# A decoder trunk's second and output products in blocks of four outputs, on 62 placements of their tiles

## The chip, the cores and the metric

The kernel runs on one core of one Trainium2 chip. The metric is the device time of one execution in microseconds: 2296.33 us is the median of three runs before the change (2295.15, 2296.38, 2296.33). The core has a matrix engine (TensorE, PE in the profile, with its weight loads listed apart as PEld), a vector engine (DVE), a scalar engine (ACT), a general engine (POOL) and SyncE, whose queue issues most DMAs. Each works through its own instructions in order and waits for the others on semaphores.

## The reference, cut to what matters

Two layers on 256 tokens of width 2048, in float32. Layer 0 has a convolution module, layer 1 an attention; each is followed by a gated feed-forward (ConvFFN).

```python
def conv_ffn(h, up_w, dw_w, dw_b, down_w):
    u = causal_depthwise_conv(h @ up_w, dw_w, dw_b)
    gt, val = jnp.split(u, 2, axis=-1)
    return (jax.nn.silu(gt) * val) @ down_w

for i in range(DEPTH):
    ...
    y = conformer_conv_module(...) if i % 2 == 0 else stick_breaking_mixer(h, sb_qkv_w[j], sb_o_w[j])
    x = x + gate * y
    ...
    x = x + gate * conv_ffn(h, ffn_up_w[i], ffn_dw_w[i], ffn_dw_b[i], ffn_down_w[i])
return rms_norm(x, final_norm_g)
```

The two products that matter here are the one with `down_w` (5632 to 2048, the "second product" of a feed-forward) and the one with the attention's output weights (2048 to 2048, the "output product").

## The kernel before, in words

Activations lie transposed: a tile has 128 features on the partitions and 256 tokens along them. An activation is kept as two halves whose sum is the float32 value, a high one (`hh`, `gh`, `oh`) and a low one (`hl`, `gl`, `ol`), in one tile with the second half some elements behind the first. A weight block of 128 by 128 is split likewise on the chip into `wh` (a cast on ACT, L244) and `wl` (a subtraction on DVE, L248), eight blocks (a piece) at a time, from `raw`, which SyncE's queue loads. Four pairs `wh`, `wl` are in rotation.

A product is a list of steps (output block, input tile), made by `plan` and packed in that order on the host. A step of the form used here has two matmuls: L299 takes `wh` against both halves of a tile at once (512 columns, through an access pattern of two runs of 256 that lie a fixed distance apart), L300 takes `wl` against the high half (256 columns). The high half's sums stand in the first 256 columns of a PSUM bank, the low half's in the rest. One output block in each second product (`LAST`, number 15) uses three matmuls of 256 instead (L304 to L306).

`plan(nbs, kts, first)` runs the first `first` outputs together, tile by tile, so that each tile is used by `first` steps running; the last four tiles (`stagger`) then go output by output, so that the outputs end four steps apart. All further outputs come one after the other, each over all its tiles. For the second products, each in two halves of 22 tiles (`down00`, `down01` in layer 0, `down10`, `down11` in layer 1), and the output product (`o`, 16 tiles), `first` is 4: four outputs together, then twelve alone.

Accumulators are PSUM banks of a pool `acc` with five buffers (tile `ps`), which serve in rotation; a bank is free again when its output is drained. In a second product the drain `down_done` copies the second half on ACT (L1024), adds it to the residual `x` on POOL (L1025) and adds the first half on DVE (L1029), which ends the bank's use. Output 14 takes both halves on DVE (L1027, L1029). In the output product both are DVE's (L1210). Where a normalization follows (`down01`, `o`, `down11`), a square (ACT, L402), a running sum of squares (POOL, L406), and either a pair of casts for the next product (ACT L458, DVE L459) or a scale (ACT, L1035) belong to the drain. The mean of squares is made on TensorE from that sum and from the last square (L410, L411).

Beside all this run reductions of the modulation weights on DVE (L338, 128 by 2048 elements each, input `mraw`), paced by pieces of the products; they occur in layer 0's second products and not in those of layer 1. A scheduler puts the instructions of each engine into a fixed order before the run, by its own estimates, with the drains at a raised priority; the order on an engine need not be that of the code.

`halved` allocates a tile for two halves. `PAIRS` gives the distance of the halves and the size of a tile, in elements of 4 bytes. By it all `g` tiles (inputs of the second products, 23 buffers) start at the same place in a stretch of 256 bytes, byte 160, and their second halves 32 bytes further on; `o` tiles alternate between the bytes 160 and 32; the `h` tiles of the other products, from `h_tiles`, rotate through 32, 96, 160 and 224.

Of the kernel before, what the change touches and what calls it, by code (L numbers as in the profile page):

```python
# [11 lines left out]
F32R = mybir.dt.float32r  # L12
# [4 lines left out]
P = 128  # L17
# [7 lines left out]
LATE_POOL, LATE_PE = 10, 8  # L25
PRODUCTS = 11

PAIRS = {"z": (264, 528, 0), "g0": (264, 576, 0), "g1": (264, 576, 0), "o": (264, 544, 0)}
HEAD = 16
UBUFS = 9  # L30
M0 = 6
# [10 lines left out]
QUIET = 6  # L42
PRIORITY = 100
MORE_MODS = 2


def plan(nbs, kts, first, stagger=4):

    seq = []
    if first > 1:  # L50
        head, nbs = nbs[:first], nbs[first:]
        s = min(stagger, len(kts) // 2)
        seq += [(n, k) for k in kts[:len(kts) - s] for n in head]
        seq += [(n, k) for n in head for k in kts[len(kts) - s:]]
    return seq + [(n, k) for n in nbs for k in kts]


class Cfg:
    def __init__(self, D, T, H, F, CW, FW):
        self.D, self.T, self.H, self.F, self.CW, self.FW = D, T, H, F, CW, FW  # L60
        KD = self.KD = D // P
        KF = self.KF = F // P
        self.GH = 4
        self.rows0 = min(ROWS, KD // 4)

        def columns(items):
            cols, n = {}, 0
            for name, k in items:
                cols[name] = (n, n + k)
                n += k  # L70
            return cols, n

        items = []
        items += [("mix_g1", KD), ("mix_b1", 3 * KD)]
        for i in range(2):
            items += [(f"ffn_g{i}", KD), (f"ffn_b{i}", 3 * KD)]
        for i in range(2):
            items += [(f"fdw{i}", 2 * KF * FW), (f"fdb{i}", 2 * KF)]
        items += [("fin_g", KD)]
        self.cols, self.ncols = columns(items)  # L80
        items = [("c", KD), ("mix_g0", KD), ("mix_b0", 3 * KD), ("pw1_b", 2 * KD), ("cdw", KD * CW), ("cdb", KD), ("ln_g", KD), ("ln_b", KD),
                 ("pw2_b", KD)]
        self.ccols, self.nccols = columns(items)

        kd = list(range(KD))
        pl = {}
        pairs = [n for j in range(KD) for n in (j, j + KD)]
        pl["pw1"] = plan(pairs, kd, min(HEAD, 2 * KD), 0)
        pl["pw2"] = plan(kd, kd, 8)
        self.halves = [list(range(KF // 2)), list(range(KF // 2, KF))]  # L90
        for i in range(2):
            for h, js in enumerate(self.halves):
                up = [n for j in js for n in (j, j + KF)]
                if h == 0:
                    pl[f"up{i}0a"] = plan(up[:FIRST], kd, FIRST, STAGGER)
                    pl[f"up{i}0b"] = plan(up[FIRST:], kd, 2, STAGGER)
                else:
                    pl[f"up{i}1a"] = plan(up[:2], kd, 1)
                    pl[f"up{i}1b"] = plan(up[2:], kd, 1)
                pl[f"down{i}{h}"] = plan(kd, js, 4)  # L100
        GH = self.GH
        for g in range(H // GH):
            hs = list(range(g * GH, (g + 1) * GH))
            qk = [n for h in hs for n in (h, H + h)]
            pl[f"qk{g}a"] = plan(qk[:FIRST], kd, FIRST if g == 0 else 1, STAGGER)
            pl[f"qk{g}b"] = plan(qk[FIRST:], kd, 1)
            pl[f"v{g}"] = [(2 * H + h, k) for k in kd for h in hs]
        pl["o"] = plan(kd, list(range(H)), 4)
        self.plans = pl
        order = ["pw1", "pw2", "up00a", "up00b", "up01a", "down00", "up01b", "down01"]  # L110
        for g in range(H // GH):
            order += [f"qk{g}a", f"v{g}"] if g == 0 else [f"v{g}", f"qk{g}a"]
            order.append(f"qk{g}b")
        self.order = order + ["o", "up10a", "up10b", "up11a", "down10", "up11b", "down11"]
# [3 lines left out]
def hybrid_trunk(ctx: ExitStack, tc: tile.TileContext, cfg: Cfg, io: dict):  # L118
    nc = tc.nc
    D, T, H = cfg.D, cfg.T, cfg.H  # L120
# [243 lines left out]
    HP = T + 8  # L364
# [7 lines left out]
    def h_pairs():  # L372
        return [pairs[k] for k in range(KD)]

    ahead_of = {kind: v[2] for kind, v in PAIRS.items()}

    def halved(pool, kind, name):

        low, size, _ = PAIRS[kind]
        at = ahead_of.pop(kind, 0)  # L380
        v = pool.tile([P, at + size], F32R, name=name)[:, at:at + 2 * low].rearrange("p (a t) -> p a t", a=2)[:, :, :T]
        return v[:, 0], v[:, 1], v

    def split_act(t, hh, hl, bias=None):
# [120 lines left out]
    with ExitStack() as cv:  # L505
# [342 lines left out]
        for c in range(KD + 1):  # L848
# [6 lines left out]
            if c > 0:  # L855
                old = [(c - 1, k) for k in vector_taps(c - 1)[split(c - 1):]]
                n = max(len(taps), len(old))
# [3 lines left out]
            for s in range(nd):  # L861
# [17 lines left out]
                if c == KD and s == 0:  # L879
                    low = split_next(later=True)  # L880
# [100 lines left out]
    def ffn(i, entry, out):  # L981
# [3 lines left out]
        with ExitStack() as fs:  # L985
            gpool = fs.enter_context(tc.tile_pool(name=f"g{i}", bufs=1))
            if i == 0:
                more["pool"] = fs.enter_context(tc.tile_pool(name="mods", bufs=MORE_MODS))
            gh, gl, gb = [None] * KF, [None] * KF, [None] * KF
# [60 lines left out]
    def mods1(parts, ring):  # L1050
# [26 lines left out]
        while ahead:  # L1077
# [4 lines left out]
    fill.append(mods1((("ffn0", 2), ("mix1", 1), ("mix1", 0), ("mix1", 2), ("ffn1", 1), ("ffn1", 0)),  # L1082
                      lambda: [mpool] * 3 + [more["pool"]] * MORE_MODS))
    entry1 = Entry("mix1")
# [143 lines left out]
    for h in range(2):  # L1228
        t = slice(h * HT, (h + 1) * HT)
        nc.vector.reciprocal(rs[:, t], std[:, t])  # L1230
        v = mpool.tile([P, D], F32, name="mraw")[:, :KD * HT].rearrange("p (k t) -> p k t", k=KD)
# [129 lines left out]
```

## Time and profile before

| what | value |
|---|---|
| median of three runs | 2296.33 us |
| the profiled execution | 2295.19 us, of which its span 2293.5 us |
| granted clock of TensorE, mean | 0.998 |
| second products (330 steps and 22 of `LAST` each) | 665.7 to 787.9, 1023.1 to 1149.6, 1801.0 to 1923.2, 2158.4 to 2280.6 us |
| output product (256 steps) | 1449.0 to 1540.8 us |
| DMA share in 665.7 to 787.9 | 0.94 |
| DMA share in 2158.4 to 2280.6 | 0.51 |

A row of a timeline gives start and length in us, engine, line, operation and what it writes from what. Names are without buffer numbers. A matmul's length is longer than its share of TensorE, since the next one starts before its end; the distance from start to start is its cost. In a row of windows stand the window, its length, busy time of PE, PEld, DVE, ACT and POOL with the count of instructions in brackets, TensorE's granted clock, the DMA share and GB/s.

### The profile page before, as it was taken

The numbers are of one execution on the slowest core, as the hardware profiler recorded it, in microseconds if no ns is written. First come the engines' busy times: TensorE is split into PE (matmuls) and PEld (weight loads), VectorE is DVE, ScalarE is ACT, GpSimd is POOL, SyncE is SP. The second block draws the span as 40 slices with busy tenths as digits, with TensorE's granted clock in tenths as the row PEclk, the third lists the DMA queues.
The fourth block names the chain that finished last, engine by engine and source line by source line (L and its number), as shares of the span: only waits on it lengthen the run. The fifth ranks groups of instructions, "written<-read, shape, count | busy, mean of one in ns | idle before, by whom it ended". The sixth has DMA issues, their size and how long they took to land.

```text
span 2293.5 us, 37839 instructions
## 1 busy us (share of the span) xinstructions
PE 2259.2 (99%) x14466; PEld 2011.7 (88%) x14466; DVE 1790.7 (78%) x2504; ACT 1218.8 (53%) x1930; POOL 410.7 (18%) x534
## 2 busy tenths in 40 slices
PE   7999999999999999999999999999999999999997
PEld 5888678999998999998898888888888888888887
DVE  7689968989998899999975555779899755777654
ACT  2056655755544455554465555657555544555553
POOL 4058713200003100003411100112000010000031
PEclk9999999999999999999999999999999999999999
DMA  9988798789899989888755555566777566656663
GB/s 397 417 336 305 273 363 349 290 298 337 332 350 340 338 329 340 336 333 307 277 185 159 165 174 169 170 189 235 240 282 277 193 191 188 190 185 186 192 192 111
DMA packets 139144, 603.16 MB, mean 263 GB/s; under 512 B 15441, under 2 KB 15569, under 8 KB 115153
## 3 DMA queue, kind: packets, MB, share of 16 engines
q1 hardware_dynamic: 120242, 464.42, 57.7%
q0 software_dynamic: 18720, 136.32, 16.0%
q8 instruction: 113, 1.85, 0.3%
q14 instruction: 69, 0.57, 0.1%
HBM read 598.58 MB, written 2.10 MB: 262 GB/s over the span
## 4 chain that ended last, share of the span: by engine, by line
PE 86%; DVE 7%; DMA 4%; ACT 1%; issue 1%; POOL 0%; DVEq 0%; SPq 0%; ACTq 0%; POOLq 0%
PE ps L299 32%; PE ps L300 16%; PE ps L304 9%; PE ps L305 9%; PE ps L306 8%; PE ps L694 5%; DMA mraw<-in_mt_mix 3%; DVE mraw L338 3%; DVE wl L248 2%; PE ps L1184 1%; PE ps L1185 1%; PE ps L1186 1%; PE ps L586 1%; DMA mraw<-in_mt_ffn 1%; DMA raw<-in_w_pw 1%
## 5 line engine op out<-in xcount | busy, mean ns | idle before, releaser
L248 DVE TENSOR_TENSOR wl<-raw,wh 128x1024 fp32r<-128x1024 f32 x688 | 848.0, 1239 | 299.5 <-ACT wh L244 297.7
L244 ACT CAST wh<-raw 128x1024 fp32r<-128x1024 f32 x688 | 719.0, 1047 | 660.6 <-PE ps L299 283.5
L299 PE MATMUL ps<-h,wh 128*128 128x512 f32 x1760 | 619.0, 394 | 0.0
L300 PE MATMUL ps<-h,wl 128*128 128x256 f32 x1760 | 494.0, 281 | 0.0
L299 PE MATMUL ps<-g,wh 128*128 128x512 f32 x1320 | 458.6, 393 | 0.0
L304 PE MATMUL ps<-h,wh 128*128 128x256 f32 (+1 forms) x1504 | 422.0, 281 | 0.0
L305 PE MATMUL ps<-h,wh 128*128 128x256 f32 (+1 forms) x1504 | 420.8, 280 | 0.0
L306 PE MATMUL ps<-h,wl 128*128 128x256 f32 (+1 forms) x1504 | 419.2, 279 | 0.1
L299 PEld LDWEIGHTS ps<-h,wh 128*128 128x128 f32 x1760 | 330.5, 188 | 74.5
L338 DVE CUSTOM_DVE_ANT_0 mraw<-mraw,csr 128x2048 f32<-128x2048 f32 x152 | 350.4, 2305 | 31.2 <-DMA mraw<-in_mt_mix 28.5
L300 PE MATMUL ps<-g,wl 128*128 128x256 f32 x1320 | 367.8, 279 | 2.3 <-DVE wl L248 2.2
L300 PEld LDWEIGHTS ps<-h,wl 128*128 128x128 f32 x1760 | 332.7, 189 | 0.2
L299 PEld LDWEIGHTS ps<-g,wh 128*128 128x128 f32 x1320 | 247.8, 188 | 57.8
L305 PEld LDWEIGHTS ps<-h,wh 128*128 128x128 f32 x1504 | 284.8, 189 | 0.1
L306 PEld LDWEIGHTS ps<-h,wl 128*128 128x128 f32 x1504 | 282.8, 188 | 0.7 <-DVE wl L248 0.7
L304 PEld LDWEIGHTS ps<-h,wh 128*128 128x128 f32 x1504 | 282.6, 188 | 0.1
L300 PEld LDWEIGHTS ps<-g,wl 128*128 128x128 f32 x1320 | 248.1, 188 | 4.1 <-DVE wl L248 4.1
L694 PE MATMUL ps<-h,raw 128*128 128x256 f32 x832 | 188.6, 382 | 0.0
L694 PEld LDWEIGHTS ps<-h,raw 128*128 128x128 f32 x832 | 158.0, 191 | 28.1 <-issue 5.8
L1025 POOL TENSOR_TENSOR x<-x,t 128x256 f32<-128x256 f32 x56 | 70.0, 1250 | 530.1 <-ACT t L1024 529.8
L1003 DVE SCALAR_TENSOR_TENSOR t<-t,par 128x254 f32<-128x254 f32 (+1 forms) x184 | 88.8, 483 | 46.6 <-ACT t L1000 43.7
L734 DVE SCALAR_TENSOR_TENSOR auxb<-u,cpar,auxb 128x256 f32<-128x256 f32 x297 | 121.6, 483 | 4.5 <-ACT auxb L718 3.7
(272 smaller groups left out, 2735.0 us busy)
## 6 DMA issues: line engine op xcount, KB each, us to landing
raw<-in_w_down SPq DMA_DIRECT2D x176, 512.0 KB, 4.3
mraw<-in_mt_ffn POOLq DMA_DIRECT2D x64, 1024.0 KB, 6.7
raw<-in_w_pw SPq DMA_DIRECT2D x96, 512.0 KB, 8.0
mraw<-in_mt_mix POOLq DMA_DIRECT2D x48, 1024.0 KB, 7.9
raw<-in_w_up01b SPq DMA_DIRECT2D x84, 512.0 KB, 6.8
raw<-in_w_up11b SPq DMA_DIRECT2D x84, 512.0 KB, 3.6
raw<-in_w_up00b SPq DMA_DIRECT2D x80, 512.0 KB, 6.1
raw<-in_w_up10b SPq DMA_DIRECT2D x80, 512.0 KB, 4.7
```

What stands on the lines that cost most here:

```text
L244: nc.scalar.copy(wh[:, :n], v[:, :n])
L248: nc.vector.tensor_tensor(wl[:, :n], v[:, :n], wh[:, :n].bitcast(F32), op=ALU.subtract)
L299: nc.tensor.matmul(o, wh[:, c], both[kt], start=first, stop=False, skip_group_check=True)
L300: nc.tensor.matmul(o[:, :T], wl[:, c], xh[kt], start=False, stop=left[nb] == 0, skip_group_check=True)
L304: nc.tensor.matmul(o, wh[:, c], xh[kt], start=first, stop=False, skip_group_check=halves > 0)
L305: nc.tensor.matmul(o, wh[:, c], xl[kt], start=False, stop=False, skip_group_check=halves > 0)
L306: nc.tensor.matmul(o, wl[:, c], xh[kt], start=False, stop=left[nb] == 0, skip_group_check=halves > 0)
L338: nc.vector.tensor_tensor_reduce(out=v, in0=v, in1=csr, scale=1.0, scalar=0.0, op0=ALU.mult, op1=ALU.add, accum_out=macc[:, nb:nb + 1])
L694: nc.tensor.matmul(banks[j][:, nb // KD * T:(nb // KD + 1) * T], w[:, b * P:(b + 1) * P], hf[kt], start=first, stop=left[j] == 0, skip_gro ...
L734: nc.vector.scalar_tensor_tensor(conv_ps[j], us[j % UBUFS][:, k:k + T], tap(j, k), conv_ps[j], op0=ALU.mult, op1=ALU.add)
L1003: nc.vector.scalar_tensor_tensor(y[:, s:], ps[:, :T - s], w(k), y[:, s:], op0=ALU.mult, op1=ALU.add)
L1025: nc.gpsimd.tensor_tensor(xs[nb], xs[nb], t, op=ALU.add)
```

## The change

`fours` cuts the outputs into blocks of four and plans each block with `first=4`: every block now is what only the first one was. `circuit` orders the 64 pairs (start of the first half, start of the second, in steps of 32 bytes within 256) into a closed round in which each pair begins where the one before ended; `START` deals 23 of them to layer 0's `g` tiles, 16 to the `o` tiles and 23 to layer 1's `g` tiles. Tiles that follow each other in memory follow each other in the round. The weights' packed order follows the plans; their bytes and the number of instructions stay. Lines of the changed kernel are 15 higher than before up to the tile code, 23 after it: L299 is L314, L248 is L263, L338 is L353, L1029 is L1052.

```diff
-PAIRS = {"z": (264, 528, 0), "g0": (264, 576, 0), "g1": (264, 576, 0), "o": (264, 544, 0)}
+START = {"g0": (0, 5, 5), "g1": (23, 5, 5), "o": (46, 5, 5)}
...
+def fours(nbs, kts):
+    return [x for i in range(0, len(nbs), 4) for x in plan(nbs[i:i + 4], kts, 4)]
+
+def circuit(n=8, at=5):
+    ends, path, out = {i: [(i + 3 * k) % n for k in range(n)] for i in range(n)}, [at], []
+    while path:
+        if ends[path[-1]]:
+            path.append(ends[path[-1]].pop())
+        else:
+            out.append(path.pop())
+    return list(zip(out[:-1], out[1:]))
...
-                pl[f"down{i}{h}"] = plan(kd, js, 4)
+                pl[f"down{i}{h}"] = fours(kd, js)
...
-        pl["o"] = plan(kd, list(range(H)), 4)
+        pl["o"] = fours(kd, list(range(H)))
...
-    ahead_of = {kind: v[2] for kind, v in PAIRS.items()}
+    edges, opened = circuit(), {}
     def halved(pool, kind, name):
-        low, size, _ = PAIRS[kind]
-        at = ahead_of.pop(kind, 0)
-        v = pool.tile([P, at + size], F32R, name=name)[:, at:at + 2 * low].rearrange("p (a t) -> p a t", a=2)[:, :, :T]
+        if kind == "z":
+            v = pool.tile([P, 2 * HP], F32R, name=name).rearrange("p (a t) -> p a t", a=2)[:, :, :T]
+            return v[:, 0], v[:, 1], v
+        first, at, base = START[kind]
+        n = first + int(name[1:])
+        p, q = edges[n]
+        ahead = 8 * ((p - at) % 8) if n == first else 0
+        low = T + 8 * ((q - p) % 8)
+        size = (ahead + low + T + 7) // 8 * 8
+        t = pool.tile([P, size], F32R, name=name)
+        v = bass.AP(tensor=t.tensor, offset=t.offset + ahead, ap=[list(t.ap[0]), [low, 2], [1, T]])
         return v[:, 0], v[:, 1], v
```

On TensorE, at the end of the first block of the last product (`down11`), before: the last step of output 3 (`ps_22061`), then output 4 alone (`ps_22328`) on the tiles g22, g0, g1.

```order
L299 MATMUL ps_22061<-g20_22042,wh_22206 128x512
L300 MATMUL ps_22061<-g20_22042,wl_22207 128x256
L299 MATMUL ps_22328<-g22_18667,wh_22228 128x512
L300 MATMUL ps_22328<-g22_18667,wl_22229 128x256
L299 MATMUL ps_22328<-g0_19842,wh_22228 128x512
L300 MATMUL ps_22328<-g0_19842,wl_22229 128x256
L299 MATMUL ps_22328<-g1_19952,wh_22228 128x512
```

The same place in the changed kernel, where outputs 4 to 7 (`ps_22328`, `ps_22331`, `ps_22334`, `ps_22337`) open:

```order
L315 MATMUL ps_22061<-g20_22042,wl_22207 128x256
L314 MATMUL ps_22328<-g22_18667,wh_22228 128x512
L315 MATMUL ps_22328<-g22_18667,wl_22229 128x256
L314 MATMUL ps_22331<-g22_18667,wh_22228 128x512
L315 MATMUL ps_22331<-g22_18667,wl_22229 128x256
L314 MATMUL ps_22334<-g22_18667,wh_22228 128x512
L315 MATMUL ps_22334<-g22_18667,wl_22229 128x256
L314 MATMUL ps_22328<-g0_19842,wh_22228 128x512
L315 MATMUL ps_22328<-g0_19842,wl_22229 128x256
L314 MATMUL ps_22331<-g0_19842,wh_22228 128x512
L314 MATMUL ps_22337<-g22_18667,wh_22228 128x512
```

`ps_22328` takes the bank that is fifth in rotation; `ps_22331`, `ps_22334` and `ps_22337` take the banks of the block's first three outputs, one after the other. The scheduler has put the fourth one's first matmul behind four steps and one L314; a matmul of the fourth output on the first tile thus stands behind some of the second tile.

On DVE, the drains of outputs 4 and 5 of the last product before, with splits of weights between them:

```order
L1029 SCALAR_TENSOR_TENSOR x_82<-ps_22328,v_ffn1_101,x_82 128x256
L248 TENSOR_TENSOR wl_22401<-raw_22345,wh_22400 128x1024
L248 TENSOR_TENSOR wl_22423<-raw_22367,wh_22422 128x1024
L248 TENSOR_TENSOR wl_22445<-raw_22398,wh_22444 128x1024
L1029 SCALAR_TENSOR_TENSOR x_82<-ps_22393,v_ffn1_101,x_82 128x256
```

And in the changed kernel, outputs 4 to 7:

```order
L1052 SCALAR_TENSOR_TENSOR x_82<-ps_22328,v_ffn1_101,x_82 128x256
L263 TENSOR_TENSOR wl_22565<-raw_22502,wh_22564 128x1024
L1052 SCALAR_TENSOR_TENSOR x_82<-ps_22331,v_ffn1_101,x_82 128x256
L1052 SCALAR_TENSOR_TENSOR x_82<-ps_22334,v_ffn1_101,x_82 128x256
L263 TENSOR_TENSOR wl_22603<-raw_22524,wh_22602 128x1024
L1052 SCALAR_TENSOR_TENSOR x_82<-ps_22337,v_ffn1_101,x_82 128x256
```

Drains that stood three splits apart now stand together, in the order that the first block has in both kernels.

On DVE in layer 0's first second product (`down00`), outputs 4 and 5 before (`ps_7138`, `ps_7202`), where the rows `ISA` are a reduction and the reading of its sum:

```order
L1029 SCALAR_TENSOR_TENSOR x_82<-ps_7138,v_ffn0_99,x_82 128x256
L338 ISA mraw_6972,macc_102<-mraw_6972,csr_83 128x2048
L338 ISA macc_102 128x1
L248 TENSOR_TENSOR wl_7213<-raw_7158,wh_7212 128x1024
L248 TENSOR_TENSOR wl_7235<-raw_7180,wh_7234 128x1024
L248 TENSOR_TENSOR wl_7257<-raw_7210,wh_7256 128x1024
L1029 SCALAR_TENSOR_TENSOR x_82<-ps_7202,v_ffn0_99,x_82 128x256
```

In the changed kernel, outputs 4 to 7 (`ps_7138`, `ps_7141`, `ps_7144`, `ps_7147`):

```order
L1052 SCALAR_TENSOR_TENSOR x_82<-ps_7138,v_ffn0_99,x_82 128x256
L263 TENSOR_TENSOR wl_7382<-raw_7324,wh_7381 128x1024
L1052 SCALAR_TENSOR_TENSOR x_82<-ps_7141,v_ffn0_99,x_82 128x256
L353 ISA mraw_7158,macc_102<-mraw_7158,csr_83 128x2048
L353 ISA macc_102 128x1
L263 TENSOR_TENSOR wl_7412<-raw_7346,wh_7411 128x1024
L1052 SCALAR_TENSOR_TENSOR x_82<-ps_7144,v_ffn0_99,x_82 128x256
L1052 SCALAR_TENSOR_TENSOR x_82<-ps_7147,v_ffn0_99,x_82 128x256
```

A reduction and a split stand between the drains of the block's second and third output.

## The prediction

> **What bounds the kernel.** I read the page first: the busy shares, then the chain that ended last.
>
> ```profile
> span 2293.5 us, 37839 instructions
> PE 2259.2 (99%) x14466; PEld 2011.7 (88%) x14466; DVE 1790.7 (78%) x2504; ACT 1218.8 (53%) x1930; POOL 410.7 (18%) x534
> PE 86%; DVE 7%; DMA 4%; ACT 1%; issue 1%; POOL 0%; DVEq 0%; SPq 0%; ACTq 0%; POOLq 0%
> ```
>
> TensorE sets the end: it is busy 99% of the span and is 86% of the chain. A microsecond in which it waits, or by which its matmuls get longer, is a microsecond of the whole, unless the same stage already holds a wait that swallows it. Next I read the groups by line in three stretches: the second feed-forward's second half of up-products (1923.4 to 2158.3 us, moving tiles h), its last second product (2158.4 to 2272.8, tiles g) and the output product behind its first block (1474.3 to 1540.8, tiles o).
>
> ```profile
> L299 PE MATMUL ps<-h,wh 128*128 128x512 f32 x672 | 235.2, 393 | 0.0
> ...
> L299 PE MATMUL ps<-g,wh 128*128 128x512 f32 x330 | 114.5, 393 | 0.0
> ...
> L299 PE MATMUL ps<-o,wh 128*128 128x512 f32 x192 | 66.6, 391 | 0.0
> ```
>
> TensorE has no gap there, so busy time over count is the cost of a step (L299 and L300 together): 350 ns on h, 347 on g, 347 on o. The program's addresses go with it: all g tiles start at one place (byte 160 of 256, second half 32 further), h tiles rotate through four places, o tiles through two. So the cost depends a little on the tile. The windows of the two second products of the first layer and of the last one show what else is near its limit:
>
> ```profile
> 665.70:780.10 114.40, 114.40 (x663) 99.85 (x662) 98.08 (x98) 50.91 (x59) 28.25 (x32) 1.00 0.93 348
> 1023.10:1141.80 118.70, 116.41 (x663) 100.36 (x662) 113.47 (x125) 60.37 (x90) 44.59 (x40) 1.00 0.81 295
> 2158.40:2272.80 114.40, 114.40 (x662) 99.86 (x661) 58.62 (x60) 62.48 (x88) 27.79 (x27) 1.00 0.55 167
> ```
>
> In the second row DVE is busy 113.5 of 118.7 us and TensorE idles 2.3 us. In the third DVE has half its time free.
>
> **The change, part by part.** No instruction is added or removed; weights arrive in another packed order, as many bytes. Three things move.
>
> **1. What a step costs on 62 tiles.** 4 products of 330 steps go from one place to 62; so do the 192 output steps behind the first block: 1512 steps that cost 347 ns now. Most run four times on one tile. Before shows such runs in the first block of the output product; here are the starts of o6, o7 and of what follows:
>
> ```profile
> 1458.81 0.40 PE L299 MATMUL ps<-o,wh 128*128 128x512 f32 x1
> ...
> 1460.19 0.40 PE L299 MATMUL ps<-o,wh 128*128 128x512 f32 x1
> ...
> 1461.62 0.34 PE L1131 MATMUL auxb<-mh,tri_r 128*128 128x384 f32 x1
> ```
>
> Four steps on o6 (start 160, as g) take 1.38 us, 345 each; four on o7 (start 32) take 1.43, 357.5 each. Only these two repeated places and the rotating four are seen, of 62, so the mean is bounded from both sides by them: 345 gives 1512 x -2 ns = -3.0 us, 357.5 gives +15.9. I take 352, the middle of g's 347 and o7's 357.5: 1512 x 5 ns = **+7.6 us**.
>
> The Trainium skill, "TensorE: Matmul & The Clock Gate", section "Back-to-back issue gap", gives a warm matmul N/2.4 + 2.5 ns with no term for where the operand lies: 215.8 and 109.2, an estimate of 325 ns a step on every tile. By that rule this term is nil and the sum 2311.6 instead of 2319.2; the rows above, 345 beside 357.5 in neighbouring runs, already disagree.
>
> **2. Waits for banks between blocks.** With five accumulators in rotation and four open at once, the second, third and fourth output of a block take the banks of the block just ended. Before opened one output at a time, with 7.6 us (22 steps) between, and never waited. Its first block is however the same four-output block, drained in the order that every block now has, so the time at which its third output (n2) is drained, after S, the start of the next output's first matmul, can be held against the place where the change first needs that bank. That place is counted from the changed order on TensorE: in the last product four steps and one L299, 4 x 0.347 + 0.231 = S+1.62; in the second layer's first second product S+1.05 (three steps); in the first layer 11 steps, S+3.83, and 16.7, S+5.79; in the output product S+1.74, later 2.08. The last product:
>
> ```profile
> 2188.05 1.10 POOL L1025 TENSOR_TENSOR x<-x,t 128x256 f32<-128x256 f32 x1 [1.68 <-ACT t L1024]
> 2188.93 0.39 PE L299 MATMUL ps<-g,wh 128*128 128x512 f32 x1
> 2189.18 0.48 DVE L1029 SCALAR_TENSOR_TENSOR x<-ps,v_ffn,x 128x256 f32<-128x256 f32 x1 [0.64 <-POOL x L1025]
> 2189.70 0.42 ACT L402 ACTIVATE t<-x 128x256 f32<-128x256 f32 x1 [1.33 <-DVE x L1029]
> 2190.03 0.46 ACT L1024 ACTIVATE t<-ps,v_ffn 128x256 f32<-128x256 f32 x1
> ...
> 2190.20 0.73 POOL L406 TENSOR_TENSOR sumsq<-sumsq,t 128x256 f32<-128x256 f32 x1 [1.05 <-ACT t L402]
> ...
> 2190.89 0.73 POOL L1025 TENSOR_TENSOR x<-x,t 128x256 f32<-128x256 f32 x1
> 2191.66 0.48 DVE L1029 SCALAR_TENSOR_TENSOR x<-ps,v_ffn,x 128x256 f32<-128x256 f32 x1 [1.99 <-POOL x L1025]
> ```
>
> S is 2188.93. n1 is drained at 2189.66 (S+0.73, needed at S+0.70). n2 is done on TensorE since 2187.71, but its copy stands on ACT behind the square of n1, then on POOL behind the sum, so its bank is free at 2192.14, S+3.21: 1.6 us late, at three boundaries **4.8**. In the first half's second product (no squares) and in the output product:
>
> ```profile
> 1831.52 0.39 PE L299 MATMUL ps<-g,wh 128*128 128x512 f32 x1
> 1832.48 0.48 DVE L1029 SCALAR_TENSOR_TENSOR x<-ps,v_ffn,x 128x256 f32<-128x256 f32 x1 [0.22 <-POOL x L1025]
> ...
> 1474.25 0.39 PE L299 MATMUL ps<-o,wh 128*128 128x512 f32 x1
> ...
> 1475.87 0.86 DVE L1210 SCALAR_TENSOR_TENSOR x<-ps,v_mix,x 128x256 f32<-128x256 f32 x2
> ```
>
> There n2's bank is free at S+1.44 against S+1.05: 0.4 x 3 = **1.2**. Output product: S+2.10 (first of the two) against 1.74, 0.4; at the later boundaries one drain of n3 (0.48) stands ahead, 2.58 against 2.08, 0.5 twice: **1.4**. The two entries behind four-blocks (up of the second layer, first queries and keys) open four banks too: the rows give 2.58 against 2.14, and n1's drain plus two of 0.48, S+1.9, against S+1.26: **1.0** together. In the first layer a modulation reduction (L338) stands between n1 and n2:
>
> ```profile
> 696.20 0.39 PE L299 MATMUL ps<-g,wh 128*128 128x512 f32 x1
> ...
> 696.85 3.00 DVE L338 CUSTOM_DVE_ANT_0 mraw<-mraw,csr 128x2048 f32<-128x2048 f32 x1
> ...
> 699.78 1.75 DVE L248 TENSOR_TENSOR wl<-raw,wh 128x1024 fp32r<-128x1024 f32 x1
> 701.46 0.86 DVE L1029 SCALAR_TENSOR_TENSOR x<-ps,v_ffn,x 128x256 f32<-128x256 f32 x2
> 702.25 2.28 DVE L338 CUSTOM_DVE_ANT_0 mraw<-mraw,csr 128x2048 f32<-128x2048 f32 x1
> ...
> 1051.06 0.48 DVE L1029 SCALAR_TENSOR_TENSOR x<-ps,v_ffn,x 128x256 f32<-128x256 f32 x1 [0.63 <-POOL x L1025]
> ...
> 1053.58 0.39 PE L299 MATMUL ps<-g,wh 128*128 128x512 f32 x1
> ...
> 1055.94 0.96 DVE L459 SCALAR_TENSOR_TENSOR h<-x,a_mix,h 128x256 fp32r<-128x256 f32 x1
> 1056.82 3.24 DVE L338 CUSTOM_DVE_ANT_0 mraw<-mraw,csr 128x2048 f32<-128x2048 f32 x1
> ...
> 1059.99 1.21 DVE L248 TENSOR_TENSOR wl<-raw,wh 128x1024 fp32r<-128x1024 f32 x1
> 1061.13 0.47 DVE L1029 SCALAR_TENSOR_TENSOR x<-ps,v_ffn,x 128x256 f32<-128x256 f32 x1
> ```
>
> First product: n2 free at 701.93, S+5.73 against 3.83: 1.9 at two boundaries, and 0.4 at the third, which has no reduction: **4.2**. Second: S+8.02 less the split of 1.21 that no longer stands ahead, 6.8 against 5.79: 1.0; nothing at the second boundary (no reduction there). At the third, n0's drain ends at S-2.0, then come a reduction (2.28), a cast of h (0.96) and n1's drain (0.48), S+1.7 against its place S+0.93: 0.8; two splits, a cast and n2's drain add 3.9, S+5.6 against 4.05 + 0.8: 0.8 again. That is 2.6. The 2.3 us that TensorE idles there already comes from late splits, which a halted TensorE lets catch up; I count half, **1.3**. Queued behind the waiting matmul is all of TensorE, and then the weight casts, which wait for it.
>
> Together 13.9 us. Bounds: 6.0 if only the second layer's products wait; 22.5 if every first-layer boundary is as late as the latest row (S+8.02).
>
> **3. The end.** Now the last four outputs end within 4.2 us, not 7.6 apart, and the final mean of squares waits for their sums on POOL:
>
> ```profile
> 2280.60 0.59 PE L410 MATMUL auxb<-sumsq,ones_d 128*128 128x256 f32 x2
> 2281.85 0.70 PE L411 MATMUL auxb<-t,ones_d 128*128 128x256 f32 x2 [0.65 <-ACT t L402]
> ```
>
> Before, L411 starts 1.25 us after the last product. By the chain of 2188 to 2192 n13 is drained at +0.73, three more drains end at +2.1; the sums of n13 and n14 (0.73 to 1.13 each) end at about +3.4, L410 takes 0.59: L411 starts at +4.0 instead of +1.25. I take **+2.5** (1.5 if the drains alone decide, 2.8 by the chain). The two inner means of squares stand 6 us behind their products, past such a chain's +4.0: nothing.
>
> **Sum.** 7.6 + 13.9 + 2.5 = 24.0 us. The profiled execution took 2295.2 us (span 2293.5 and 1.7 around it), 1.1 under the median of the three, 2296.3. Forecast: 2319.2 us, 1.1% slower.
>
> **Rivals.** *Tiles cost the same* (347 as now): only waits and end, 2311.6. For it: the three stretches lie within 347 to 350; against: o7. *The waits dissolve*: drains come earlier, because after each wait DVE and ACT have caught up, and only tiles and end remain, 2305.3. For it: DVE is half idle in the second layer; against: n2 there waits for a chain of ACT, POOL and DVE, not for a busy engine. *DVE falls behind* in the first layer: two drains, reductions and splits bunch up, the splits run late and TensorE waits for weights as well; upper waits, 2295.2 + 7.6 + 22.5 + 2.5 = 2327.8, and with 357.5 ns a step 2336. *The other side, faster*: most of the 62 places are cheaper than any seen. It pays for waits and end, 16.4 us, from 1512 x 11 ns on, a mean step under 336 ns; at 332 it gives 2295.2 - 22.7 + 16.4 = 2288.9. For it: even starts were never run in L299; against: no place seen in a run of equal tiles is under 345. That the change does not do what it says is excluded by its order and addresses: 62 pairs of places, blocks of four.
>
> **How the numbers follow.** Forecast 0.55 (2312 to 2328), equal tiles 0.13, dissolved waits 0.12, DVE behind 0.13, cheap tiles 0.07. A change of 0.2% (4.6 us) is what a measurement of this kernel can tell from none. Faster: 0.04, out of the last; same: 0.05, the rest of it and the low end of dissolved waits; slower 0.91. The bounds together reach from 2295.2 - 3.0 + 6.0 + 1.5 = 2300 to 2295.2 + 15.9 + 22.5 + 2.8 = 2336; the range 2301 to 2337 holds all but cheap tiles and the far end of the third rival.
>
> **What would show it.** TensorE's idle time in the waits view, named after the drain L1029 (L1052 in the changed numbering) or L1210, some 14 us at 15 boundaries and 2 entries, with n2's place in the order; steps of 347 to 358 ns by tile between them, repeating for the same tile in both products of a layer; the first L411-like matmul 4 us behind the last product. It is wrong if runs on even starts take under 336 ns, or if the boundaries show no gap.

## The result and the profile after

| | before | after |
|---|---|---|
| median | 2295.74 us (2295.15 to 2296.38, 4 runs) | 2322.03 us (2321.48 to 2323.31, 4 runs) |
| profiled execution, its span | 2295.2, 2293.5 | 2321.5, 2319.8 |

The ratio is 1.0115 (95% interval 1.0102 to 1.0128): 26.3 us slower, inside the range of the prediction and 2.3 us behind its 24.0. The page of the changed kernel, the three lines that answer to the first three of before:

```profile
span 2319.8 us, 37838 instructions
PE 2270.9 (98%) x14466; PEld 2017.8 (87%) x14466; DVE 1783.7 (77%) x2504; ACT 1219.4 (53%) x1930; POOL 396.1 (17%) x534
PE 62%; DVE 3%; POOL 1%; ACT 1%; issue 1%; POOLq 0%; DVEq 0%; ACTq 0%
```

TensorE's busy time grew by 11.7 us (2270.9 against 2259.2), the span by 26.3; the other 14.6 are new idle time. The next rows say whom TensorE waits for, by the view of waits from the first second product to the end of the last one (microseconds, times, longest), before and then after; two more waits, 0.7 us together, are the same in both.

```profile
PE ps L300 <- DVE wl L248: 2.2, 4, 0.7
```

```profile
PE ps L314 <- DVE x L1052: 10.5, 9, 1.7
PE ps L319 <- DVE x L1052: 2.8, 3, 1.3
PE ps L314 <- DVE x L1233: 1.3, 3, 0.5
PE ps L319 <- DVE x L1233: 0.6, 1, 0.6
```

Late splits of weights (L248) are gone; in their place stand 15.2 us behind drains of accumulators, L1052 in the second products and L1233 in the output product. The view counts a matmul as busy to its modelled end, so a wait begins late in it. From start to start, less the usual 0.232 us behind a wide matmul and 0.117 behind its narrow one, the waits come to 20.4 us in the five products and 1.9 at the two entries behind them, against 4.3 before (0.5 us of both stands in the output product's first block and is no wait for a bank). The second products in windows (busy time of PE, PEld, DVE, ACT, POOL; clock; DMA share), here from the first to the last of their matmuls:

```profile
665.80:793.82 128.02, 124.54 (x729) 108.96 (x728) 103.60 (x102) 53.35 (x61) 27.80 (x32) 1.00 0.91 336
1029.02:1157.82 128.80, 124.59 (x729) 108.88 (x727) 111.16 (x126) 63.65 (x90) 32.90 (x38) 1.00 0.78 287
2174.03:2304.19 130.16, 125.06 (x728) 108.76 (x726) 58.05 (x60) 61.63 (x86) 22.96 (x26) 1.00 0.46 146
```

The clock is full in each, and DVE is half idle in the last, which is the longest: not a busy engine but a chain makes TensorE wait. The timeline at the first boundary of the last product shows it. S, the start of the next block's first matmul, is 2204.93; n0 to n3 are the four outputs of the block that has just ended.

```profile
2204.93 0.40 PE L314 MATMUL ps<-g,wh 128*128 128x512 f32 x1
...
2205.13 0.48 DVE L1052 SCALAR_TENSOR_TENSOR x<-ps,v_ffn,x 128x256 f32<-128x256 f32 x1 [0.62 <-POOL x L1048]
2205.64 0.42 ACT L425 ACTIVATE t<-x 128x256 f32<-128x256 f32 x1 [1.32 <-DVE x L1052]
2205.97 0.46 ACT L1047 ACTIVATE t<-ps,v_ffn 128x256 f32<-128x256 f32 x1
2206.14 0.74 POOL L429 TENSOR_TENSOR sumsq<-sumsq,t 128x256 f32<-128x256 f32 x1 [1.05 <-ACT t L425]
2206.47 0.39 PE L314 MATMUL ps<-g,wh 128*128 128x512 f32 x1
2206.84 0.72 POOL L1048 TENSOR_TENSOR x<-x,t 128x256 f32<-128x256 f32 x1
2207.59 0.48 DVE L1052 SCALAR_TENSOR_TENSOR x<-ps,v_ffn,x 128x256 f32<-128x256 f32 x1 [1.98 <-POOL x L1048]
2208.13 0.50 PE L314 MATMUL ps<-g,wh 128*128 128x512 f32 x1 [1.28 <-DVE x L1052]
...
2208.47 0.40 PE L315 MATMUL ps<-g,wl 128*128 128x256 f32 x2
```

It is the chain of the prediction, row by row: square of n1 on ACT, copy of n2 behind it, sum and addition on POOL, drain on DVE. The bank is free at 2208.07, S+3.14 (forecast S+3.21), and TensorE, which was through at S+1.77, starts again at S+3.20. At the next boundary n1 is late as well, here in the rows of POOL, DVE and PE:

```profile
2236.26 1.39 POOL L429 TENSOR_TENSOR sumsq<-sumsq,t 128x256 f32<-128x256 f32 x1 [1.41 <-ACT t L425]
2237.61 0.73 POOL L1048 TENSOR_TENSOR x<-x,t 128x256 f32<-128x256 f32 x1
2238.37 0.48 DVE L1052 SCALAR_TENSOR_TENSOR x<-ps,v_ffn,x 128x256 f32<-128x256 f32 x1 [1.31 <-POOL x L1048]
2238.91 0.50 PE L314 MATMUL ps<-g,wh 128*128 128x512 f32 x1 [0.56 <-DVE x L1052]
```

n0's sum takes 1.39 us on POOL, where the same line took 0.74 in the fence above, and n1's addition stands behind it. At the first boundary of the first layer's first product the reduction stands between n1 and n2, as forecast:

```profile
696.83 0.48 DVE L1052 SCALAR_TENSOR_TENSOR x<-ps,v_ffn,x 128x256 f32<-128x256 f32 x1 [0.63 <-POOL x L1048]
697.23 3.02 DVE L353 CUSTOM_DVE_ANT_0 mraw<-mraw,csr 128x2048 f32<-128x2048 f32 x1
...
700.18 1.74 DVE L263 TENSOR_TENSOR wl<-raw,wh 128x1024 fp32r<-128x1024 f32 x1
701.84 0.86 DVE L1052 SCALAR_TENSOR_TENSOR x<-ps,v_ffn,x 128x256 f32<-128x256 f32 x2
```

And the end, where the last second product ends at 2304.19:

```profile
2304.07 0.28 PE L321 MATMUL ps<-g,wl 128*128 128x256 f32 x1
...
2306.92 1.08 PE L433 MATMUL auxb<-sumsq,ones_d 128*128 128x256 f32 x2 [2.57 <-POOL sumsq L429]
...
2307.78 1.06 PE L434 MATMUL auxb<-t,ones_d 128*128 128x256 f32 x2
```

L434 starts 3.6 us behind the product (1.25 before, 4.0 forecast); from the product's end to the span's end it is 15.58 us, 12.88 before.

By stages, the 26.3 us are: down00 +5.8, down01 +2.3, output product +2.7, down10 +2.8, down11 +7.9, the two entries +1.1 and +0.8, the end +2.7; the others come to +0.1.

### The profile page after: what moved, and what is told of

Read it like the earlier page. It is cut to its first block, busy times and chain, and to the rows that moved or that the text cites. A ratio compares the mean times of both kernels' runs of the same rounds, so it can differ in the third digit from the quotient of the medians.

```text
span 2319.8 us, 37838 instructions
## 1 busy us (share of the span) xinstructions
PE 2270.9 (98%) x14466; PEld 2017.8 (87%) x14466; DVE 1783.7 (77%) x2504; ACT 1219.4 (53%) x1930; POOL 396.1 (17%) x534
## 4 chain that ended last, share of the span: by engine, by line
PE 62%; DVE 3%; POOL 1%; ACT 1%; issue 1%; POOLq 0%; DVEq 0%; ACTq 0%
PE ps L314 29%; PE ps L315 15%; PE ps L319 4%; PE ps L320 4%; PE ps L321 4%; PE ps L1208 1%; PE ps L1209 1%; PE ps L1207 1%; DVE wl L263 1%; POOL x L1048 1%; ACT wh L259 1%; POOL sumsq L429 0%; DVE h L482 0%; DVE x L1052 0%; DVE x L1233 0%
## 5 line engine op out<-in xcount | busy, mean ns | idle before, releaser
L263 DVE TENSOR_TENSOR wl<-raw,wh 128x1024 fp32r<-128x1024 f32 x688 | 842.6, 1231 | 334.0 <-ACT wh L259 332.4
L314 PE MATMUL ps<-h,wh 128*128 128x512 f32 x1760 | 618.9, 394 | 0.0
L314 PE MATMUL ps<-g,wh 128*128 128x512 f32 x1320 | 468.6, 396 | 10.8 <-DVE x L1052 10.5
L314 PEld LDWEIGHTS ps<-h,wh 128*128 128x128 f32 x1760 | 330.5, 188 | 74.2
L353 DVE CUSTOM_DVE_ANT_0 mraw<-mraw,csr 128x2048 f32<-128x2048 f32 x152 | 351.6, 2313 | 32.0 <-DMA mraw<-in_mt_mix 28.6
L314 PEld LDWEIGHTS ps<-g,wh 128*128 128x128 f32 x1320 | 247.8, 188 | 69.9 <-DVE x L1052 10.9
L1048 POOL TENSOR_TENSOR x<-x,t 128x256 f32<-128x256 f32 x56 | 56.5, 1011 | 560.1 <-ACT t L1047 559.9
```

The costliest lines, as they stand in the source:

```text
L263: nc.vector.tensor_tensor(wl[:, :n], v[:, :n], wh[:, :n].bitcast(F32), op=ALU.subtract)
L314: nc.tensor.matmul(o, wh[:, c], both[kt], start=first, stop=False, skip_group_check=True)
L353: nc.vector.tensor_tensor_reduce(out=v, in0=v, in1=csr, scale=1.0, scalar=0.0, op0=ALU.mult, op1=ALU.add, accum_out=macc[:, nb:nb + 1])
L1048: nc.gpsimd.tensor_tensor(xs[nb], xs[nb], t, op=ALU.add)
```

## The experiments

The question was what each of the three terms is worth by itself, and whether the steps are dearer because of where the tile lies or because a tile is used four times running. Each kernel is compared with the kernel before on the same chip. One thing has to be taken off when single profiles are read by stages: the pointwise stage ahead of all this (284.3 to 405.4 us before) takes 121.1, 122.7 or 124.4 us from one execution to the next, whatever the kernel; stage figures below leave it out.

**The new order on the old tiles.** The kernel before, with `fours` for the four second products and the output product:

```diff
-                pl[f"down{i}{h}"] = plan(kd, js, 4)
+                pl[f"down{i}{h}"] = fours(kd, js)
...
-        pl["o"] = plan(kd, list(range(H)), 4)
+        pl["o"] = fours(kd, list(range(H)))
```

> Blocks of four in all five products, but the tiles of the kernel before (g all at byte 160, halves 32 further; o at 160 and 32). Waits theory (banks free too late between blocks, 18 us with the two entries, and 2.7 us at the end; tiles 5.3 us): TensorE's gaps at the boundaries as in the changed kernel, g steps back at 347 ns, 2295.7 + 18 + 2.7 = 2316.5 us. Tile theory (the new places cost most of the 26 us): under 2303 us. Third possibility, four steps running on one tile are themselves dear: g steps stay at 350 ns and the time at 2322.

2321.97 us, ratio 1.0114 (1.0097 to 1.0131). By stages the profile has +24.1: the waits are those of the changed kernel (21.2 us from start to start, 20.4 there), and the end +1.95. The rest is in the steps, and not evenly: the windows of the first three blocks of down10, all on tiles at one place, have

```profile
1815.06:1845.60 30.54, 30.54 (x178) 26.66 (x177) 16.87 (x19) 14.33 (x18) 1.62 (x2) 1.00 0.68 207
1845.60:1877.20 31.60, 31.52 (x178) 27.20 (x177) 15.32 (x15) 13.28 (x15) 4.39 (x5) 1.00 0.62 183
1877.20:1908.80 31.60, 31.51 (x179) 27.27 (x178) 15.32 (x15) 13.28 (x15) 4.41 (x5) 1.00 0.57 183
```

The blocks hold the same 88 steps each, but the second and third take 1.06 us longer. About half of that is the wait for banks at their start, counted from start to start. The other half is in the steps: each there is 353.3 ns from start to start instead of 347, all the way through, and in down11 every block runs at 347 again. So four running steps on a tile at this place are not dear as such; a block runs in one of two tempos. Over the kernel the slow one costs 1.5 us (330 steps each of down00 and down10 at +1.9 and +3.9 ns in the mean, less 0.4 us in down01, which before ran three outputs at 353.3).

In the output product something else makes the steps dearer, by 0.9 us (256 steps at +3.5 ns). Its tiles lie at byte 160 and byte 32 in turn, and each of the rows below starts the four steps on one tile, o4 to o8 in the third block:

```profile
1513.80 0.39 PE L303 MATMUL ps<-o,wh 128*128 128x512 f32 x1
...
1515.19 0.40 PE L303 MATMUL ps<-o,wh 128*128 128x512 f32 x1
...
1516.62 0.39 PE L303 MATMUL ps<-o,wh 128*128 128x512 f32 x1
...
1518.01 0.40 PE L303 MATMUL ps<-o,wh 128*128 128x512 f32 x1
...
1519.44 0.39 PE L303 MATMUL ps<-o,wh 128*128 128x512 f32 x1
```

Four steps at byte 160 take 1.39 us, four at byte 32 take 1.43. In all four blocks, away from their openings and ends, it is 347 and 358 ns a step, where single outputs, which go from tile to tile, take 346.7 in the mean on the same tiles. Here, then, four running steps on a tile are dear, though on the other place they are not. The time is the one that the third possibility named, but not for its reason: g's steps are not at 350, and neither the two tempos nor the output product's part was foreseen.

**The old order on the new tiles.** The changed kernel with the two lines above undone:

```diff
-                pl[f"down{i}{h}"] = fours(kd, js)
+                pl[f"down{i}{h}"] = plan(kd, js, 4)
...
-        pl["o"] = fours(kd, list(range(H)))
+        pl["o"] = plan(kd, list(range(H)), 4)
```

> Plans of before (one block of four, then twelve outputs alone), with the 62 placements. Waits theory: no gap between outputs, steps of 350.5 ns instead of 347, 2295.7 + 5.3 = 2301 us. Tile theory: over 2312 us. If only running four times on a tile makes a place dear or cheap: steps at 347 and 2296 us.

2301.23 us, ratio 1.0019 (1.0010 to 1.0028). No wait at a boundary, no longer end; the tiles alone are worth 4.2 us by stages (1.3, 0.0, 0.7, 0.8, 1.7 in the five products, less 0.3 at an entry). By steps they are worth 5.0; down01 shows nothing of its 0.5 because its waits for splits are 0.4 us shorter here. The group of the last product, which in the kernel before was 114.5 us for 330 (the window here holds 328 of them):

```profile
L314 PE MATMUL ps<-g,wh 128*128 128x512 f32 x328 | 115.4, 396 | 0.0
```

Busy time over count is the cost of a step: 347 ns becomes 352 in this product and 349.3 to 350.5 in the other four (means from start to start).

**The changed kernel with eight banks.** The five accumulators are joined by the three banks of the two helper pools, which are free in these products:

```diff
+    EIGHT = 2 * (4 * [psum_acc] + [psum_b, psum_b, psum_a, psum_acc])
...
-            gemm(f"down{i}0", gh, gl, down_done(0), both=gb, apart=LAST)
+            gemm(f"down{i}0", gh, gl, down_done(0), both=gb, apart=LAST, banks=EIGHT)
...
-        gemm("o", oh, ol, o_done, ready=lambda kt: oh[kt] is not None, quiet=QUIET, both=ob)
+        gemm("o", oh, ol, o_done, ready=lambda kt: oh[kt] is not None, quiet=QUIET, both=ob, banks=EIGHT)
```

(`down{i}1` likewise.)

> The changed kernel, with the accumulators of the five products dealt out of all eight banks (five of acc, two auxb, one auxa) so that a block of four opens on banks that have been free for a whole block. Waits theory: the gaps at the 15 boundaries and the two entries go, 2322 - 18 = 2304 us; tiles (5.3) and end (2.7) stay. Rival, the gaps come from the drains' load on DVE, ACT and POOL, by way of late weight splits, whatever the banks: gaps of the same size, now before L315 with a split as releaser, 2318 to 2322 us.

2299.96 us, ratio 1.0015 (1.0006 to 1.0025): nearly 23 of the 26 us are gone. All that the view of waits has left, from the first second product on to 2290 us, is

```profile
PE auxb L435 <- POOL sumsq L431: 2.6, 1, 2.6
PE auxb L317 <- DVE wl L265: 0.5, 1, 0.5
PE auxb L1156 <- ACT mh L1151: 0.2, 1, 0.2
```

of which the first is the end, and the other two stand before as well. That is more than expected, because the waits for late splits in down01 do not come back with the banks: this product is 3.2 us shorter than before, though its tiles are dearer. The other products keep 1.25, 0.7, 1.3 and 1.4, the tiles' share.

**The last four outputs one at a time**, in every product of the changed kernel:

```diff
-    return [x for i in range(0, len(nbs), 4) for x in plan(nbs[i:i + 4], kts, 4)]
+    return [x for i in range(0, len(nbs) - 4, 4) for x in plan(nbs[i:i + 4], kts, 4)] + plan(nbs[-4:], kts, 1)
```

> The changed kernel, but the last four outputs of each product one after the other as before (three blocks of four, then four alone). Waits theory: the third boundary's waits (0.35 + 2.75 + 0.76 + 0.35 + 2.33 = 6.5 us), the two entries' (1.9) and the longer end (2.7) go, 2322 - 11 = 2311 us. Rival for the end (it is longer for another reason than the four drains close together): the end stays 2.7 us longer, 2313.7 us.

2312.03 us, ratio 1.0068 (1.0053 to 1.0083). The end is what it was before (12.87 us), the entries too (-0.2 and 0.0), and down11 keeps two of its three boundaries: 4.1 us of waits instead of 6.45.

**Both halves drained on DVE in the last product.** If the chain over ACT and POOL makes n2 late, a drain that goes past both must not be:

```diff
-                    if nb < KD - 2:
+                    if nb < KD - 2 and not (i == 1 and h == 1):
```

> The changed kernel; in the last product alone all outputs are drained by DVE (both halves, as output 14 is), so no copy on ACT and no addition on POOL stands in the drain. Theory (output n2's copy stands on ACT behind the square of n1, then on POOL behind the sum): that product's waits fall from 6.5 us to under 1.5, the other products stay, 2322 - 5 = 2317 us. Rival (the bank is late because DVE itself is late): the waits stay or grow with two more 0.48 us drains per block, 2322 us or more.

2314.15 us, ratio 1.0081 (1.0067 to 1.0095), 7.9 us faster than the changed kernel. The other products are as there (+5.9, +2.3, +2.7, +2.8); down11 is +1.4 instead of +7.9, with not one wait in the view, and the end +0.4 instead of +2.7. DVE's rows at the first boundary:

```profile
2205.78 0.47 DVE L1050 SCALAR_TENSOR_TENSOR x<-ps,v_ffn,x 128x256 f32<-128x256 f32 x1
2206.29 0.48 DVE L1052 SCALAR_TENSOR_TENSOR x<-ps,v_ffn,x 128x256 f32<-128x256 f32 x1
2206.69 1.22 DVE L263 TENSOR_TENSOR wl<-raw,wh 128x1024 fp32r<-128x1024 f32 x1
2207.82 1.05 DVE L1050 SCALAR_TENSOR_TENSOR x<-ps,v_ffn,x 128x256 f32<-128x256 f32 x2
2208.79 0.87 DVE L1052 SCALAR_TENSOR_TENSOR x<-ps,v_ffn,x 128x256 f32<-128x256 f32 x2
```

Both halves of two outputs now take 1.84 us (the last two rows) on one engine, with nothing between. The expectation missed that the end rests on the same chain, and was 3 us too high.

**One dear and one cheap place, in the old order.** Among the changed kernel's tiles, the mean of the steps that repeat a tile was lowest, 344.1 ns, where the first half starts at 160 of 256 bytes and the second at 0, and highest, 366.8, where they start at 96 and 160. Each of the two was given to all g tiles of the kernel before (the numbers are the distance of the halves and the tile's size, in words, and the words ahead of the first tile):

```diff
-PAIRS = {"z": (264, 528, 0), "g0": (264, 576, 0), "g1": (264, 576, 0), "o": (264, 544, 0)}
+PAIRS = {"z": (264, 528, 0), "g0": (272, 576, 48), "g1": (272, 576, 48), "o": (264, 544, 0)}
```

> The kernel before, with its plans; all g tiles start at byte 96 of 256 and their second halves at byte 160, the pair that took 366.8 ns a step in the changed kernel when run four times on one tile (356.6 over all its steps). If the pair of places decides a step's cost: 1290 steps x 9.6 to 19.8 ns = 12 to 26 us more, 2308 to 2321 us. If the neighbours of a tile or its address beyond 256 bytes decide: steps at 347 to 351, 2296 to 2301 us.

2301.49 us, ratio 1.0024 (1.0014 to 1.0033).

```diff
+PAIRS = {"z": (264, 528, 0), "g0": (280, 576, 0), "g1": (280, 576, 0), "o": (264, 544, 0)}
```

> The kernel before, with its plans; all g tiles start at byte 160 and their second halves at byte 0 of 256, the pair that took the least in the changed kernel (344.1 ns a step in runs, 345.6 over all). If the pair decides: 1320 steps x -1.2 to -2.7 ns = 1.6 to 3.6 us less than before, 2292 to 2294 us. If not: 347 to 351 ns a step, 2296 to 2301 us.

2292.26 us, ratio 0.9984 (0.9975 to 0.9993). The groups of the last product, first the dear place, then the cheap one:

```profile
L299 PE MATMUL ps<-g,wh 128*128 128x512 f32 x330 | 115.9, 395 | 0.0
```

```profile
L299 PE MATMUL ps<-g,wh 128*128 128x512 f32 x330 | 113.4, 390 | 0.0
```

Busy time over count gives 351 and 344 ns: the cheap place is cheap alone too, but the dear one is no dearer than the mean of all 62. The 366.8 was never its price. The pair (96, 160) belongs to one tile, g0 of layer 1, which is the first tile of down10 and the second of down11, and so stands where the blocks open, wait and start again. With eight banks these waits are gone and tiles and order stay; there the first four steps of down10, all on this tile, run from the first of these rows to the second:

```profile
1801.19 0.39 PE L316 MATMUL ps<-g,wh 128*128 128x512 f32 x1
...
1802.59 0.40 PE L316 MATMUL ps<-g,wh 128*128 128x512 f32 x1
```

That is 1.40 us, 350 ns each, and over the kernel the repeated steps on this tile take 351.0 there, as when the place is used alone. In that run the means by place reach from 344.8 (160 and 0) to 355.5 (0 and 64).

**The cheap place for o as well** (`"o": (280, 576, 0)` besides).

> The kernel before with the tiles of o too on the place that cost 343.4 ns a step on g (both halves on starts at the same place of 32 words, first half at byte 160, second at 256 further of 280 words). If the place alone sets a step's cost, the second products stay at 343.4 and the steps of the output product fall from 347.8 to about 344: 2291.3 us (2296 less 4.2 as with g alone, less 256 x 3.6 ns = 0.9 of o). Rival, that the products differ in themselves: o stays at 347 to 348 a step, 2292.2.

2291.06 us, ratio 0.9976 (0.9967 to 0.9985): the output product fell by 1.0 us, its steps from 347.8 ns to 343.7, as expected if the place alone sets them.

**What is left of the blocks of four** when the banks, the end and the place are taken care of: blocks of four, the last four outputs one at a time, eight banks, cheap places for g and o.

> Cheap places for g and o, blocks of four with the last four outputs one at a time, and eight banks of accumulators. If the blocks lose only by the wait for banks and by the end, nothing of the loss is left, and the splits of weights that make layer 0's second half wait 3.8 us before are gone, as in the run with eight banks: 2291.3 - 3.8 = 2287.5 us. Rival, that four runs on one tile cost something of themselves: as much above, 2290 to 2293, with steps of the second products over 343.4 where no wait stands.

2287.52 us (2285.53 to 2287.63), ratio 0.9961 (0.9948 to 0.9973): faster than both kernels, and what was expected if, at these places, the blocks lose only by banks and the end. Steps in the second products are 343.4 to 343.5 ns, so at this place four running steps on a tile cost nothing of themselves; down01 is 4.5 us shorter than before, of which some 1.1 is the place, as in the other products; 0.9 of its 3.8 us of waits is left.

**A displacement.** The two tempos remained to be explained. The kernel before, with a small matmul ahead of outputs 4 to 13 of down10:

```diff
+                if name == "down10" and first and 4 <= nb < 14:
+                    nc.tensor.matmul(psum_a()[:, :8 * (nb - 3)], wh[:, c], xh[kt][:, :8 * (nb - 3)], start=True, stop=True)
```

> The kernel before with one more matmul, of 8, 16, ... 80 columns, ahead of outputs 4 to 13 of layer 1's first second product; its result is not used. Two-tempo theory: the tempo of a run of steps is set by the moment at which it starts and is kept until something displaces it, so some of these ten outputs run at 346.7 ns a step and others at about 353, constant within an output; the product gets longer by the matmuls themselves (about 10 x 0.02 to 0.1 us) and by up to 5 x 22 x 6.6 ns = 0.7 us. Rival, that a displacement changes nothing (the second tempo belongs to the tiles or the bank): all ten at 346.7.

A single time, 2297.83 us; what counts is the timeline. The rows show output 10 (between L302 at 1879.49 and at 1886.78 lie 21 steps), the extra matmul of 64 columns, and output 11 behind it:

```profile
1879.49 0.28 PE L302 MATMUL ps<-g,wl 128*128 128x256 f32 x1
...
1886.78 0.28 PE L302 MATMUL ps<-g,wl 128*128 128x256 f32 x1
1886.89 0.19 PE L299 MATMUL auxa<-g,wh 128*128 128x64 f32 x1
1886.92 0.48 PE L301 MATMUL ps<-g,wh 128*128 128x512 f32 x1
1887.24 0.28 PE L302 MATMUL ps<-g,wl 128*128 128x256 f32 x1
...
1894.66 0.28 PE L302 MATMUL ps<-g,wl 128*128 128x256 f32 x1
```

21 steps of output 10 take 7.29 us, 347 ns each; of output 11, on the same 22 tiles, 7.42, 353 each. Of the ten outputs behind a displacement, 11 and 12 (64 and 72 columns) ran at 353.3, the rest, 13 with 80 columns among them, at 346.6; within an output every step behind the first one or two is the same. The second tempo thus belongs neither to the tile nor to the order in fours, and a displacement of TensorE's stream can switch it on and off. By what rule, no run shows.

## Why the prediction held, point by point

| term | forecast | measured in the changed kernel |
|---|---|---|
| steps on 62 places | 7.6 | 5.1 |
| waits, down00 | 4.2 | 4.6 |
| waits, down01, less the splits that fall away | 1.3 | 1.6 (5.4 less 3.8) |
| waits, output product | 1.4 | 2.0 |
| waits, two entries | 1.0 | 1.9 |
| waits, down10 | 1.2 | 1.4 |
| waits, down11 | 4.8 | 6.45 |
| end | 2.5 | 2.7 |
| sum | 24.0 | 25.8 |

Measured are, for the steps, the mean from start to start less that of before, times their count; for the waits, what stands over it. The stages' 26.3 hold 0.5 more. That the sum came so near is in part luck: the steps were put 2.5 us too high and the waits 4.1 too low.

**The steps: the size was off, by half.** The 352 ns were the middle between g's 347 and o7's 357.5. The changed kernel's mean is 350 to 351, and the term 5.1 us; the old order on the new tiles has 5.0. The reading of o7 was right: tiles at byte 32 take 358 in every block of the new order on the old tiles. The step that failed is the one from two places to 62: o7's price lies above that of every place that the run with eight banks shows under running steps (at most 355.5), so a middle that leans on it is too high. The other bound, o6's 345, is a matter of rounding: four such steps take 1.39 us, 347 each, in the rows above. Nor is the place the whole of a price: the output product's tiles cost 346.7 in the mean when single, and those at byte 32 cost 358 in fours, and a place that took 347 took 353 behind a displacement. The rule of the Trainium skill ("TensorE: Matmul & The Clock Gate", "Back-to-back issue gap"), by which the term is nil and which the page calls the gap of an isolated matmul, does not agree with these runs: 343.4 against 351.1 ns with nothing but the place changed. Nor do they bear out the rival of steps under 336: the lowest mean seen is 343.4. A cheap place there is, though, and one for all tiles does better than 62.

**The waits: the mechanism was right, their size low by 4.1 us.** At down11's first boundary n2 came 0.07 us from where it was forecast; eight banks took all waits away, the drain on DVE those of down11. Three things were missing. A wait of TensorE costs more than its own length: the first narrow matmul behind it starts 0.34 us behind the wide one instead of 0.23 (2208.13 and 2208.47 in the last product), about 0.1 at each. Then n1 was read off the first boundary and taken as in time at all three; at the second and third its addition stands behind a longer sum on POOL, 0.6 us each. And at down01's second boundary nothing was forecast, since no reduction stands there; there the same n1 is late by 1.2, behind its addition on POOL, and at the third both n1 and n2 are (1.7 and 0.9, forecast 0.8 each). Why the entries cost 1.9 instead of 1.0 was not followed up. The forecast's upper bound of the waits, 22.5, does not come out of its own condition: with all six boundaries of the first layer at S+8.02 they are 3 x 4.19 and 3 x 2.23, which with 8.4 for the rest is 27.7. The measured 18.0 lies under both.

**down01 was right by two errors.** Bank waits of 2.6 us were taken to come, and half of that to be made up by late splits that fall away. All the split waits fell away (3.8 us from start to start), and 5.4 of bank waits came. It is not the halts that cure the split waits, since with eight banks the product has no waits at all. Whether the blocks of four do it or the banks was not tried apart. For the blocks speaks the run with blocks of four, eight banks and cheap places: what is left there of split waits, 0.9 us between 1126.9 and 1136.1, lies among the last four outputs, which run one at a time. Why is open.

**The end** was read right, as to the chain and nearly to the size: L434 at +3.6 us, forecast +4.0. Single last outputs take it away, and drains past POOL nearly so (+0.4).

**The rivals.** The waits did not dissolve, though DVE is half idle in the second layer: the reason given against it, a chain and not a busy engine, is what the drain on DVE shows. DVE did not fall behind in the first layer; no split was late in its second products. The parts are not additive: the order alone makes +24.1 us by stages, the tiles alone +4.2, both +26.3. The 2 us between are near the 2.5 of dearer steps that the new order met on the old tiles, 1.5 by the slow tempo and 0.9 on o tiles at byte 32. With both changes the steps cost 5.1 us in all, as with the tiles alone. That is arithmetic; why the slow tempo does not come on top there, no run shows.

## What to carry to other kernels

With N accumulators in rotation and k opened at once, k - (N - k) of a block's banks are those of the block that has just ended; compare the place in the program where each is first needed with the time at which the chain of engines that drains it comes round to it, at more than one boundary, since a slower neighbour shifts it. Idle banks of other pools were worth some five times more here than the best place tried. And before a layout is spread over many places, measure one fixed place by itself: the better of the two tried was 4 us better, the 62 together 4 us worse. When one place or tile looks dear in a mean, see first whether waits stand on it.

## What the runs showed of the hardware

- A step of a 512- and a 256-column matmul costs 343.4, 346.7 or 351.1 ns in the mean of 330, by the place of the moving tile's halves (bytes 160 and 0, 160 and 192, 96 and 160 of 256).
- At 160 and 192 it has two tempos: the same tiles ran at 346.6 ns, behind displacements by matmuls of 64 and 72 columns at 353.3, and behind one of 80 at 346.6 again. What the state is stays open. At 160 and 0 no second tempo was seen; the steps went back to 343.4 behind each of the five waits for splits in down01.
- At byte 32 the order counts: four running steps on such a tile took 358 ns each, and 346.7 in the mean when every step went to the next tile and the tiles lay at byte 160 and byte 32 in turn.
- POOL's sum of 128x256 took 0.74 us with DVE idle (2206.14) and 1.39 beside a split on DVE (2235.83 to 2237.06); beside a reduction, in down01 (1122.37 to 1124.65), 2.20. In both cases it ended 0.6 us behind the end of the instruction on DVE.
- The pointwise stage takes 121.1, 122.7 or 124.4 us in different executions of like code. The times of the kernel before gather near 2295, 2296.5 and 2298 us, at like distances, so this stage may be most of their scatter; only one execution of each kernel was traced, so that is not shown.
